# Other values for loads and engine instructions in the planner of a two-layer decoder trunk

## The chip, the cores and the metric

The kernel runs on one core of a Trainium2 chip. The metric is the device time of one execution in microseconds, the median of several runs. One further execution was recorded by the hardware profiler; all rows below come from it. PE is TensorE, DVE VectorE, ACT ScalarE, POOL GpSimd, SP SyncE; PEld is PE's loading of weights.

## What is computed

Two layers over x (1024 tokens of 1024 channels, f32), each with a mixing part and an MLP, both normalised and modulated by six vectors (shift, scale, gate, twice) that come from a conditioning vector c. The last line of the function is a final norm.

```python
for l in range(DEPTH):                                   # DEPTH = 2
    mod = (silu(c) @ w_ada[l] + b_ada[l])                # 6 x 1024
    shift1, scale1, gate1, shift2, scale2, gate2 = split(mod)
    h = rms_norm(x, g_mix_norm[l]) * (1.0 + scale1) + shift1
    p = h @ w_in[l]          # q_sb, k_sb, v_sb, q_lat, kv_lat, k_rope, gate_sb, gate_mla
    o_sb  = stick_breaking_attention(q_sb, k_sb, v_sb) @ w_sb_out[l]     # 8 heads of 64
    o_mla = softmax_attention(latent q, k, v with rope) @ w_mla_out[l]   # 8 heads
    merged = sigmoid(gate_sb) * o_sb + sigmoid(gate_mla) * o_mla
    x = x + gate1 * (merged @ w_mix_out[l])
    h = rms_norm(x, g_mlp_norm[l]) * (1.0 + scale2) + shift2
    x = x + gate2 * (square(relu(h @ w_up[l])) @ w_down[l])
```

## The kernel before

Products are made in a 32-bit float type with reduced mantissa. Each f32 operand is split into a high and a low part: ACT casts the high part, POOL or DVE subtracts it from the source for the low one, and PE sums three products (high by high, high by low, low by high). x and all hidden values lie with channels on the 128 partitions and tokens along the free dimension, in halves of 512; a product is 128 channels by 512 tokens. The MLP uses a seven-product scheme for 2 x 2 blocks in place of eight, with additions of blocks on DVE.

The stages of a layer are: modulation vectors (`mac` on DVE multiplies blocks `AD` of `w_ada` by c and adds them up in `A`; PE sums `A` over partitions), the input projection (`parts` are its split weights, `H` the split input, `lt`, `lh`, `ll` the latent vectors), attention (`sq` and `mq` are queries and keys, `sc` the scores, `W` and `F` the weights, which PE transposes into `wth` and `wtl`, `V` the values), merge and output projection, MLP up (`pr` loaded weights, `T` sums of their blocks made by `pair_weights`, `pw` their split parts, `u` and `hid` the hidden values, combined on DVE by `combine`, line 1525), and MLP down (`down`, line 1582). The values of the attention go to HBM as rows `T`, come back as `vT` by one load of 512 KB, and are transposed on PE (`make_v`, line 975).

In `down`, `operand` loads the weights `wr` (512 KB each) and eight hidden blocks `T` (256 KB each, in six buffers shared with other uses); ACT casts each `T` into `bo`, DVE subtracts for its low half and so frees the `T`. For each step and each p, DVE adds or subtracts `wr` blocks where the step needs it, ACT casts `wr` into the high `ws`, POOL subtracts for the low `ws`, and PE runs 24 products on the pair. DVE adds the result into `x`. There are 14 steps of 4 pairs in each layer, 112 pairs in all.

What sets the order: nothing is issued as it is written. `Plan.record` (line 193) notes each operation with its reads, writes, tiles and duration (`cost`, line 442). `deadlines` (line 264) lays PE's operations end to end in the order of the code and counts back from them: an operation is due when its earliest user is due, less its own duration, a latency between the engines and a margin; later tiles that will take a tile's buffer count as users too. `schedule` (line 299) then plays the program with these durations, in time: whenever an engine is free it starts, of the operations that are ready and have their buffers, the one that is due first. `emit` (line 423) issues all operations in order of their planned start. On the chip each engine runs its instructions in that order and waits on semaphores, so a planned duration never sets a time on the chip, only an order. All loads and stores go through SP's one queue, in order. All instructions carry line 218, the inner function of `record`.

Of the kernel before, what the change touches and what calls it, by code (L numbers as in the profile page):

```python
# [176 lines left out]
class Plan:  # L177
# [15 lines left out]
    def record(self, engine, method, a, k):  # L193
# [14 lines left out]
        op.early = self.early  # L208
        op.func = str(k.get("func", "")).split(".")[-1]
        op.dur = cost(op.eng, method, a, k, outs, ins)  # L210
        op.succs, op.news, op.tiles = [], [], []
        if op.eng == "PE":
# [51 lines left out]
    def deadlines(self):  # L264
        ops = self.ops
        t = 0.0
        back = []
        for op in ops:
            back.append(t)
            if op.eng == "PE":  # L270
                op.dl = t
                t += op.dur
            else:
                op.dl = None
        soft = {}
        for t_ in self.tiles:
            c = t_.cls
            if not c.slots:
                continue
        for c in {id(t_.cls): t_.cls for t_ in self.tiles if t_.cls.slots}.values():  # L280
            q = len(c.slots)
            for i in range(len(c.tiles) - q):
                nxt = c.tiles[i + q].ops[0]
                for o in c.tiles[i].ops:
                    if o < nxt:
                        soft.setdefault(o, []).append(nxt)
        for op in ops:
            for p in op.preds:
                ops[p].succs.append(op.i)
        for op in reversed(ops):  # L290
            d = back[op.i] + 60.0
            for s in op.succs + soft.get(op.i, []):
                s = ops[s]
                x = s.dl - op.dur - self.lat(op, s) - (1.2 if op.eng == "DMA" else 0.3)
                d = min(d, x)
            if op.eng != "PE":
                op.dl = d - op.early

    def schedule(self):
        self.deadlines()  # L300
        ops = self.ops
        n = len(ops)
# [52 lines left out]
        now = 0.0  # L355
        while done < n:
# [7 lines left out]
            now = heapq.heappop(events)  # L364
            while events and events[0] <= now + 1e-6:
                heapq.heappop(events)
            for e in engines:
                while free[e] <= now + 1e-6:
# [5 lines left out]
                    while av and len(skipped) < 60:  # L374
                        d, i = heapq.heappop(av)
                        op = ops[i]
# [10 lines left out]
                    op = pick  # L387
# [4 lines left out]
                    dur = op.dur  # L392
# [6 lines left out]
                    end = now + dur  # L399
                    if e == "DMA":  # L400
                        busy = max(0.46, dur)
                        end = now + 1.2 + dur
                    op.end = end
                    free[e] = now + busy
                    heapq.heappush(events, free[e])
# [8 lines left out]
                    for s in op.succs:  # L414
                        s = ops[s]
# [15 lines left out]
def width(v):  # L431
    n = 1
    if v.dims is not None:
        for a, b in [(x, y) for _, x, y in v.dims[1:]]:
            n *= b - a
        return n
    for a, b in v.box[1:]:
        n *= b - a
    return n


def cost(eng, method, a, k, outs, ins):

    if eng == "DMA":
        v = (outs + ins)[0]
        n = 1
        for x, y in v.box:
            n *= y - x
        return n * 4 / 360e3
    n = width(outs[0])  # L450
    if eng == "PE":
        dt = str(ins[0].tile.dtype)
        if "32r" in dt:
            return 0.107 if n < 16 else (n if n >= 256 else 4 * n) / 2400.0 + 0.003
        if "bfloat" in dt:
            return n / 2400.0 + 0.003
        return 0.109 if method == "transpose" else 0.13
    psum = any(getattr(v.tile.cls, "psum", False) for v in ins)
    if eng == "ACT":
        x = 0.052 if psum else 0.093  # L460
        if isinstance(k.get("bias"), View):
            x += 0.093
        if k.get("accum_out") is not None:
            x += 0.093
        return x + n / 1200.0
    if eng == "DVE":
        if method == "reduce_max":
            n = width(ins[0])
        x = 0.069 + n / 960.0
        if method == "tensor_tensor_scan":  # L470
            x += n / 960.0
        if method == "scalar_tensor_tensor" and len(ins) > 2:
            x += 0.06
        if method in ("tensor_scalar", "tensor_copy") and not psum:
            x = 0.069 + n / 1920.0 + (0.06 if len(ins) > 1 else 0)
        return x
    if method == "memset":
        return 0.036 + n / 1200.0
    if method == "tensor_scalar":
        return 0.26 + n * 3.33e-3  # L480
    return 0.15 + n * 2.1e-3


class Part:
# [1289 lines left out]
```

## Time and profile before

| | us |
|---|---|
| three runs | 3214.45, 3218.63, 3219.18 |
| median | 3218.63 |
| the profiled execution | 3226.48 |
| its span, first to last instruction | 3224.7 |
| PE busy | 3079.3 (95%) |
| DVE busy | 2242.2 (70%) |
| ACT busy | 1542.2 (48%) |
| POOL busy | 1184.0 (37%) |
| mean granted TensorE clock | 0.986 |

Busy time of an engine is time in which it has an instruction in work. A row that gives a wait counts idle time of an engine in front of an instruction, with the operation that ended last before it. The share of PE says how little of the span is not products; the rows below say where that little lies.

### The profile page before, as it was taken

Reading aid. Unit: us, or ns where it says so; the run is one execution under the profiler, and the core shown is the slowest. Engines: PE = TensorE matmul, PEld = TensorE weight load, DVE = VectorE, ACT = ScalarE, POOL = GpSimd, SP = SyncE. Lnnn points to the kernel's source line nnn. Section 1 sums busy time; section 2 is a strip of 40 time slices with the busy share of each in tenths; the row PEclk is TensorE's granted clock in tenths of the full one; section 3 lists DMA queues with packets and bytes.
Section 4 is the critical chain, followed back from the end, with each engine's and each line's share of the span. In section 5 each row is a group of like instructions: output and inputs, shape, how many; then the busy total and the mean of one; then the engine's idle time right before and its main releaser. Section 6 shows DMA issues by size and latency. Waiting matters only on the chain.

```text
span 3224.7 us, 42818 instructions
## 1 busy us (share of the span) xinstructions
PE 3079.3 (95%) x14791; PEld 2497.0 (77%) x14791; DVE 2242.2 (70%) x3246; ACT 1542.2 (48%) x2647; POOL 1184.0 (37%) x942
## 2 busy tenths in 40 slices
PE   5999999999999899999999999999999999999998
PEld 4877777888777778877777777778877777887786
DVE  7585556667667966698878636556756677559886
ACT  4443556667344444433443336556744444444343
POOL 3322444211233655344432324441113355434442
PEclk9999999999999999999999999999999999999999
DMA  6559445445843644845144764454466445476622
GB/s 220 176 184 280 142 117 138 111 106 169 273 136 111 221 164 163 280 153 184 66 140 133 246 207 131 113 143 115 121 201 195 134 141 183 150 225 212 183 85 86
DMA packets 439869, 527.20 MB, mean 163 GB/s; under 512 B 32339, under 2 KB 310501, under 8 KB 439653
## 3 DMA queue, kind: packets, MB, share of 16 engines
q1 hardware_dynamic: 439652, 524.48, 53.0%
q8 instruction: 117, 1.92, 0.2%
q14 instruction: 100, 0.81, 0.1%
HBM read 362.36 MB, written 162.00 MB: 163 GB/s over the span
## 4 chain that ended last, share of the span: by engine, by line
PE 60%; DVE 16%; DMA 12%; issue 5%; ACT 5%; POOL 1%; SPq 1%; DVEq 0%; ACTq 0%; POOLq 0%
PE pp L218 47%; PE tp L218 8%; PE sc L218 4%; DVE A L218 3%; DMA T<-dram 3%; DVE bo L218 2%; DMA dram<-T 2%; DVE T L218 2%; DMA AD<-in_w_ada 2%; DVE x L218 1%; DVE wr L218 1%; DMA dram<-lt 1%; ACT F L218 1%; ACT W L218 1%; DVE F L218 1%
## 5 line engine op out<-in xcount | busy, mean ns | idle before, releaser
L218 PE MATMUL pp<-H,parts 128*128 128x512 f32 x4000 | 1052.9, 406 | 13.6 <-DVE T L218 5.9
L218 PEld LDWEIGHTS pp<-H,parts 128*128 128x128 f32 x4000 | 733.0, 190 | 165.0 <-DVE T L218 6.8
L218 PE MATMUL pp<-bo,ws 128*128 128x512 f32 x2688 | 635.3, 397 | 19.0 <-POOL ws L218 12.6
L218 PEld LDWEIGHTS pp<-bo,ws 128*128 128x128 f32 x2688 | 506.5, 189 | 145.5 <-POOL ws L218 17.0
L218 POOL TENSOR_TENSOR parts<-raw,parts 128x1024 fp32r<-128x1024 f32 (+2 forms) x158 | 320.4, 2029 | 686.6 <-ACT parts L218 609.8
L218 POOL TENSOR_TENSOR ws<-wr,ws 128x1024 fp32r<-128x1024 f32 x112 | 298.3, 2672 | 370.2 <-ACT ws L218 352.1
L218 PE MATMUL pp<-t,pw 128*128 128x512 f32 x1344 | 322.9, 399 | 18.3 <-ACT u L218 11.2
L218 PEld LDWEIGHTS pp<-t,pw 128*128 128x128 f32 x1344 | 255.3, 191 | 80.6 <-ACT u L218 12.2
L218 DVE TENSOR_TENSOR wtl<-tp,wth 128x512 fp32r<-128x512 f32 (+3 forms) x384 | 207.3, 550 | 68.0 <-ACT wth L218 65.8
L218 DVE TENSOR_TENSOR_SCAN F<-F,sc 128x128 f32<-128x128 f32 (+7 forms) x128 | 171.2, 1347 | 109.3 <-ACT F L218 77.9
L218 ACT CAST parts<-raw 128x1024 fp32r<-128x1024 f32 (+2 forms) x158 | 140.6, 891 | 211.4 <-PE pp L218 174.6
L218 PE MATMUL pp<-b,pw 128*128 128x512 f32 x1008 | 239.7, 395 | 0.0
L218 DVE SCALAR_TENSOR_TENSOR x<-pp,const,x 128x512 f32<-128x512 f32 x256 | 180.5, 741 | 81.1 <-PE pp L218 81.1
L218 ACT CAST bo<-T 128x512 fp32r<-128x512 f32 x224 | 134.6, 619 | 206.5 <-DMA T<-dram 149.5
L218 DVE TENSOR_TENSOR bo<-T,bo 128x512 fp32r<-128x512 f32 x224 | 218.5, 1022 | 17.1 <-ACT bo L218 16.6
L218 ACT CAST wth<-tp 128x512 fp32r<-128x512 f32 (+3 forms) x384 | 181.1, 481 | 100.6 <-PE tp L218 94.4
L218 DVE SCALAR_TENSOR_TENSOR A<-AD,const,A 128x256 f32<-128x256 f32 x280 | 196.6, 702 | 45.6 <-DMA AD<-in_w_ada 40.4
L218 POOL TENSOR_TENSOR W<-W,F 128x127 f32<-128x127 f32 (+7 forms) x128 | 153.1, 1203 | 198.8 <-ACT W L218 102.3
L218 PEld LDWEIGHTS pp<-b,pw 128*128 128x128 f32 x1008 | 189.0, 188 | 45.2 <-DVE u L218 0.4
L218 POOL TENSOR_TENSOR pw<-T,pw 128x512 fp32r<-128x512 f32 x112 | 163.4, 1477 | 164.7 <-ACT pw L218 164.7
L218 PE MATMUL tp<-const,W 128*128 128x128 f32 x1152 | 183.5, 273 | 4.2 <-DVE wtl L218 4.2
L218 PE MATMUL pp<-merged,parts 128*128 128x512 f32 x768 | 182.0, 398 | 5.8 <-POOL parts L218 2.9
(155 smaller groups left out, 4534.4 us busy)
## 6 DMA issues: line engine op xcount, KB each, us to landing
T<-dram SPq DMA_DIRECT2D x352, 256.0 KB
dram<-T SPq DMA_DIRECT2D x208, 256.0 KB
dram<-u SPq DMA_DIRECT2D x92, 512.0 KB
AD<-in_w_ada SPq DMA_DIRECT2D x160, 256.0 KB
raw<-in_w_in SPq DMA_DIRECT2D x68, 512.0 KB
wr<-in_w_down SPq DMA_DIRECT2D x64, 512.0 KB
pr<-in_w_up SPq DMA_DIRECT2D x56, 512.0 KB
sq<-dram SPq DMA_DIRECT2D x96, 256.0 KB
```

Source lines behind the costliest of these rows:

```text
L218: getattr(getattr(nc, engine), method)(*[r(x) for x in a], **{n: r(x) for n, x in k.items()})
```

## The change

Eight numbers of the planner take other values: the fixed part of a transfer in `deadlines` and `schedule` (1.2 to 2.2 us), the rate of a transfer in `cost` (360 to 280 GB/s), and the fixed parts of ACT, DVE and POOL instructions. The duration of PE's operations and the latencies between engines stay.

```diff
@@ deadlines, line 294
-                x = s.dl - op.dur - self.lat(op, s) - (1.2 if op.eng == "DMA" else 0.3)
+                x = s.dl - op.dur - self.lat(op, s) - (2.2 if op.eng == "DMA" else 0.3)
@@ schedule, line 402
-                        end = now + 1.2 + dur
+                        end = now + 2.2 + dur
@@ cost, DMA, line 449
-        return n * 4 / 360e3
+        return n * 4 / 280e3
@@ cost, ACT, line 460
-        x = 0.052 if psum else 0.093
+        x = 0.13 if psum else 0.17
@@ cost, DVE, lines 469 and 475
-        x = 0.069 + n / 960.0
+        x = 0.13 + n / 960.0
...
-            x = 0.069 + n / 1920.0 + (0.06 if len(ins) > 1 else 0)
+            x = 0.13 + n / 1920.0 + (0.06 if len(ins) > 1 else 0)
@@ cost, POOL, line 481
-    return 0.15 + n * 2.1e-3
+    return 0.25 + n * 2.1e-3
```

The program has the same instructions as before but for the merging of some neighbours. Of the planner's 14775 operations on PE 6546 stand at another place in its order, on ACT 1339 of 2486, on DVE 2020 of 3246, on POOL 330 of 938, of 1763 transfers 1128. The three places below are those that the prediction speaks of. A row is one instruction: operation, output, inputs, elements, and "x2" for several alike in a row. In a name such as `ws_5414_27068` the first number is the planner's tile and is the same in both programs; the second numbers the creation and is not.

**Layer 1, down projection, ACT**, before:

```order
L218 CAST ws_5405_26932<-wr_5357_26663 128x1024
L218 CAST ws_5408_26969<-wr_5358_26711 128x1024
L218 CAST bo_5390_26978<-T_5389_26857 128x512
L218 CAST bo_5392_26985<-T_5391_26867 128x512
L218 CAST bo_5394_26991<-T_5393_26875 128x512
L218 CAST bo_5396_26997<-T_5395_26881 128x512
L218 CAST bo_5398_27003<-T_5397_26887 128x512
L218 CAST bo_5400_27009<-T_5399_26893 128x512
L218 CAST ws_5411_27021<-wr_5359_26769 128x1024
L218 CAST bo_5402_27039<-T_5401_27012 128x512
L218 CAST bo_5404_27046<-T_5403_27018 128x512
L218 CAST ws_5414_27068<-wr_5360_26809 128x1024
```

and now:

```order
L218 CAST ws_5408_26948<-wr_5358_26778 128x1024
L218 CAST ws_5411_26992<-wr_5359_26896 128x1024
L218 CAST bo_5390_27012<-T_5389_26973 128x512
L218 CAST bo_5392_27022<-T_5391_26981 128x512
L218 CAST bo_5394_27031<-T_5393_26988 128x512
L218 CAST bo_5396_27039<-T_5395_26999 128x512
L218 CAST ws_5414_27046<-wr_5360_26930 128x1024
L218 CAST bo_5398_27058<-T_5397_27008 128x512
L218 CAST bo_5400_27065<-T_5399_27017 128x512
L218 CAST bo_5402_27083<-T_5401_27044 128x512
L218 CAST bo_5404_27094<-T_5403_27055 128x512
L218 CAST ws_5433_27100<-wr_5357_26730 128x1024
```

The cast of `ws_5414` moved ahead of four casts `bo`, that of `ws_5411` ahead of all six.

**The same place, DVE**, before:

```order
L218 TENSOR_TENSOR bo_5404_27046<-T_5403_27018,bo_5404_27046 128x512
L218 TENSOR_TENSOR wr_5359_26769<-wr_5295_26359,wr_5359_26769 128x1024
L218 TENSOR_TENSOR wr_5360_26809<-wr_5296_26447,wr_5360_26809 128x1024
L218 TENSOR_TENSOR wr_5326_26521<-wr_5326_26521,wr_5358_26711 128x1024
L218 SCALAR_TENSOR_TENSOR x_5268_26532<-pp_5410_27070,const_2132_10135,x_5268_26532 128x512 x2
L218 TENSOR_TENSOR wr_5327_26558<-wr_5327_26558,wr_5359_26769 128x1024
L218 TENSOR_TENSOR wr_5328_26586<-wr_5328_26586,wr_5360_26809 128x1024
L218 TENSOR_TENSOR wr_5273_26235<-wr_5273_26235,wr_5357_26663 128x1024
L218 SCALAR_TENSOR_TENSOR x_5270_26572<-pp_5413_27116,const_2132_10135,x_5270_26572 128x512 x2
L218 TENSOR_TENSOR bo_5418_27161<-T_5417_27057,bo_5418_27161 128x512
L218 TENSOR_TENSOR bo_5420_27168<-T_5419_27063,bo_5420_27168 128x512
```

and now:

```order
L218 TENSOR_TENSOR bo_5404_27094<-T_5403_27055,bo_5404_27094 128x512
L218 SCALAR_TENSOR_TENSOR x_5268_26574<-pp_5410_27048,const_2132_10155,x_5268_26574 128x512 x2
L218 TENSOR_TENSOR wr_5359_26896<-wr_5295_26422,wr_5359_26896 128x1024
L218 TENSOR_TENSOR wr_5360_26930<-wr_5296_26487,wr_5360_26930 128x1024
L218 SCALAR_TENSOR_TENSOR x_5270_26693<-pp_5413_27096,const_2132_10155,x_5270_26693 128x512 x2
L218 TENSOR_TENSOR wr_5325_26520<-wr_5325_26520,wr_5357_26730 128x1024
L218 TENSOR_TENSOR bo_5418_27152<-T_5417_27091,bo_5418_27152 128x512
L218 TENSOR_TENSOR bo_5420_27160<-T_5419_27104,bo_5420_27160 128x512
L218 TENSOR_TENSOR wr_5326_26563<-wr_5326_26563,wr_5358_26778 128x1024
L218 SCALAR_TENSOR_TENSOR x_5272_26743<-pp_5416_27143,const_2132_10155,x_5272_26743 128x512 x2
L218 TENSOR_TENSOR bo_5422_27168<-T_5421_27111,bo_5422_27168 128x512
```

`wr_5326` moved from ahead of `bo_5418` to behind it, as did `wr_5327`, `wr_5328` and `wr_5273`, which come after these rows; `wr_5325` moved from some 25 places earlier to just ahead of it. On SP's queue the load of `wr_5505` moved from ahead of the load of `T_5429`, the source of the cast `bo_5430`, to eight places further on.

**Layer 0, attention, PE**, where the product `pp_1051` is made whose result goes to HBM and returns as `vT_1060`, before:

```order
L218 MATMUL pp_1051_4835<-H_18_658,parts_1036_4467 128x512
L218 MATMUL tp_1049_4901<-wth_1041_4747,V_914_4345 128x256 x4
L218 MATMUL tp_1049_4901<-wtl_1040_4846,V_912_4337 128x256 x4
L218 MATMUL tp_1049_4901<-wtl_1042_4776,V_914_4345 128x256 x4
L218 MATMUL pp_1051_4835<-H_19_671,parts_1035_4451 128x512 x2
L218 MATMUL pp_1051_4835<-H_19_671,parts_1036_4467 128x512
L218 MATMUL pp_1051_4835<-H_20_680,parts_1035_4451 128x512 x2
L218 MATMUL pp_1051_4835<-H_20_680,parts_1036_4467 128x512
L218 MATMUL pp_1051_4835<-H_21_703,parts_1035_4451 128x512 x2
L218 MATMUL pp_1051_4835<-H_21_703,parts_1036_4467 128x512
L218 MATMUL pp_1051_4835<-H_22_717,parts_1035_4451 128x512 x2
L218 MATMUL pp_1051_4835<-H_22_717,parts_1036_4467 128x512
```

and now, from the last product of `pp_1051`:

```order
L218 MATMUL pp_1051_4819<-H_22_713,parts_1036_4386 128x512
L218 MATMUL sc_1057_4916<-sq_1055_4728,sq_1054_4464 128x256
L218 MATMUL sc_1057_4916<-sq_1056_4751,sq_1054_4464 128x256
L218 LDWEIGHTS const_2_82
L218 MATMUL sc_1057_4916<-const_4_80,const_2_82 128x128
L218 MATMUL sc_1065_4920<-sq_1055_4728,sq_1054_4464 128x256
L218 MATMUL tp_1048_4925<-const_1_65,W_1031_4809 128x128 x4
L218 MATMUL sc_1065_4920<-sq_1056_4751,sq_1054_4464 128x256
L218 LDWEIGHTS const_2_82
L218 MATMUL sc_1065_4920<-const_4_80,const_2_82 128x128
L218 MATMUL pp_1081_4935<-H_7_298,parts_1079_4675 128x512 x2
L218 MATMUL tp_1049_4941<-wth_1039_4870,V_912_4332 128x256 x4
```

The transposes `tp_1048` and the sixteen products `tp_1049` moved from ahead of the end of `pp_1051` to behind it. The transposes of `vT_1060` follow 44 rows behind the end of `pp_1051` before, 47 now; they stand three products earlier than before.

**Layer 0, MLP up, DVE**, where the hidden blocks `u_2157`, `u_2158`, `u_2172` and `u_2173` are combined and the sums `T_2205` to `T_2208` of loaded weights `pr` are made, before:

```order
L218 TENSOR_TENSOR T_2205_10480<-pr_2203_10379,pr_2204_10450 128x512
L218 TENSOR_TENSOR T_2206_10487<-T_2205_10480,pr_2203_10379 128x512
L218 TENSOR_TENSOR T_2207_10494<-pr_2203_10379 128x512
L218 TENSOR_TENSOR u_2158_10360<-u_2158_10360,u_2157_10314 128x512
L218 TENSOR_TENSOR T_2208_10509<-pr_2204_10450,T_2206_10487 128x512
L218 TENSOR_TENSOR u_2157_10314<-u_2157_10314 128x512
L218 TENSOR_TENSOR u_2173_10474<-u_2173_10474,u_2172_10434 128x512
L218 TENSOR_TENSOR u_2157_10314<-u_2158_10360,u_2157_10314 128x512
L218 TENSOR_TENSOR u_2172_10434<-u_2172_10434 128x512
L218 TENSOR_TENSOR u_2158_10360<-u_2158_10360,u_2157_10314 128x512
L218 TENSOR_TENSOR u_2172_10434<-u_2173_10474,u_2172_10434 128x512
L218 TENSOR_TENSOR u_2173_10474<-u_2173_10474,u_2172_10434 128x512
```

and now:

```order
L218 TENSOR_TENSOR u_2158_10363<-u_2158_10363,u_2157_10313 128x512
L218 TENSOR_TENSOR u_2157_10313<-u_2157_10313 128x512
L218 TENSOR_TENSOR u_2173_10466<-u_2173_10466,u_2172_10420 128x512
L218 TENSOR_TENSOR u_2172_10420<-u_2172_10420 128x512
L218 TENSOR_TENSOR u_2157_10313<-u_2158_10363,u_2157_10313 128x512
L218 TENSOR_TENSOR u_2172_10420<-u_2173_10466,u_2172_10420 128x512
L218 TENSOR_TENSOR u_2158_10363<-u_2158_10363,u_2157_10313 128x512
L218 TENSOR_TENSOR T_2205_10545<-pr_2203_10433,pr_2204_10499 128x512
L218 TENSOR_TENSOR u_2173_10466<-u_2173_10466,u_2172_10420 128x512
L218 TENSOR_TENSOR T_2206_10552<-T_2205_10545,pr_2203_10433 128x512
L218 TENSOR_TENSOR T_2207_10554<-pr_2203_10433 128x512
L218 TENSOR_TENSOR T_2208_10558<-pr_2204_10499,T_2206_10552 128x512
```

The four steps on `T` moved behind seven of the eight steps of the combine.

**The same place, SP**, before:

```order
L218 DMA pr_2204_10450<-in_w_up 128x4x256
L218 DMA dram_2070_10462<-u_2158_10360 128x1024
L218 DMA u_2173_10474<-dram_2067_9881 128x1024
L218 DMA AD_2313_10489<-in_w_ada 128x2x256
L218 DMA dram_2070_10462<-u_2157_10314 128x512
L218 DMA pr_2230_10506<-in_w_up 128x4x256
```

and now:

```order
L218 DMA dram_2070_10450<-u_2158_10363 128x1024
L218 DMA u_2173_10466<-dram_2067_9888 128x1024
L218 DMA u_2172_10420<-dram_2067_9888 128x512
L218 DMA dram_2070_10450<-u_2157_10313 128x512
L218 DMA pr_2204_10499<-in_w_up 128x4x256
L218 DMA dram_2070_10450<-u_2157_10313 128x1024
```

The load of `pr_2204` moved from ahead of two writes of `u` and two other transfers to behind the first write of `u_2157`.

## Rows read from the trace of the kernel before

**Rows 1.** The page, busy us (share of the span) and instructions of each engine.

```profile
PE 3079.3 (95%) x14791; PEld 2497.0 (77%) x14791; DVE 2242.2 (70%) x3246; ACT 1542.2 (48%) x2647; POOL 1184.0 (37%) x942
```

**Rows 2.** Table by stretch: start:end us, length, busy us and instructions, PEclk, DMA share, GB/s.

```profile
240.00:320.00 80.00, 73.95 (x325) 59.68 (x325) 50.13 (x91) 25.52 (x49) 23.25 (x27) 0.98 0.90 277
...
2700.00:2780.00 80.00, 80.00 (x346) 64.72 (x346) 51.64 (x65) 34.75 (x49) 42.65 (x30) 1.00 0.49 167
...
2960.00:3040.00 80.00, 74.72 (x312) 59.18 (x311) 75.52 (x79) 30.06 (x40) 42.04 (x14) 0.98 0.67 201
```

**Rows 3.** Waits of PE: engine, line, waited for, us in total, times, longest us.

```profile
PE pp L218 <- POOL ws L218: 12.6, 10, 2.4
PE pp L218 <- ACT u L218: 11.2, 3, 9.2
...
PE tp L218 <- DMA vT<-dram: 10.1, 7, 2.2
PE tp L218 <- ACT A L218: 8.2, 7, 2.1
PE pp L218 <- ACT pw L218: 7.0, 2, 3.9
...
PE sc L218 <- ACT W L218: 4.9, 12, 0.6
```

**Rows 4.** Chain of waits around 530 us: start us, us, what.

```profile
520.33 1.88 PE tp L218 x16
...
530.33 6.36 DMA dram<-T
...
536.70 3.98 DMA vT<-dram
```

**Rows 5.** The tile `bo`: instructions, duration ns min/median/max, first and last start us.

```profile
L218 ACT CAST bo<-T x224: 600/621/627, 1306.7 to 3171.9; 128x512 fp32r<-128x512 f32 x112
L218 DVE TENSOR_TENSOR bo<-T,bo x224: 672/680/2926, 1307.4 to 3173.8; 128x512 fp32r<-128x512 f32 x112
```

**Rows 6.** Timeline of ACT, layer 1 down: start us, us, instruction [idle before <-releaser].

```profile
2962.70 1.32 ACT L218 CAST bo<-T 128x512 fp32r<-128x512 f32 x2 [10.84 <-DMA T<-dram]
...
2975.77 1.05 ACT L218 CAST ws<-wr 128x1024 fp32r<-128x1024 f32 x1
...
2989.83 1.37 ACT L218 CAST bo<-T 128x512 fp32r<-128x512 f32 x2 [13.01 <-DMA T<-dram]
```

**Rows 7.** Chain of waits at the same place, GpSimd's subtraction.

```profile
2992.22 3.05 POOL ws L218
```

**Rows 8.** Timeline of PE at the same place.

```profile
2968.99 3.27 PE L218 MATMUL pp<-bo,ws 128*128 128x512 f32 x13 [1.46 <-POOL ws L218]
...
2992.20 0.73 PE L218 MATMUL pp<-bo,ws 128*128 128x512 f32 x2 [1.12 <-ACT ws L218]
2995.32 2.97 PE L218 MATMUL pp<-bo,ws 128*128 128x512 f32 x7 [2.39 <-POOL ws L218]
```

**Rows 9.** Timeline of DVE at the same place.

```profile
2979.17 4.40 DVE L218 TENSOR_TENSOR wr<-wr,wr 128x1024 f32<-128x1024 f32 x3
```

**Rows 10.** Timeline of PE in attention, the transposes of `vT`.

```profile
540.73 1.09 PE L218 MATMUL tp<-const,vT 128*128 128x128 f32 x8 [1.60 <-DMA vT<-dram]
```

**Rows 11.** Timeline of PE in MLP up, layer 0.

```profile
1091.37 2.92 PE L218 MATMUL pp<-t,pw 128*128 128x512 f32 x6 [9.16 <-ACT u L218]
```

**Rows 12.** Timeline of DVE at the same place.

```profile
1078.00 0.69 DVE L218 TENSOR_TENSOR T<-pr,pr 128x512 f32<-128x512 f32 x1 [2.08 <-DMA pr<-in_w_up]
1078.72 0.69 DVE L218 TENSOR_TENSOR T<-T,pr 128x512 f32<-128x512 f32 x1
```

**Rows 13.** Timeline of SP at the same place.

```profile
1078.13 0.32 SPq L218 DMA_DIRECT2D dram<-u  x1
```

**Rows 14.** Chain of waits at the same place, the second load `pr`.

```profile
1072.19 5.79 DMA pr<-in_w_up
```

**Rows 15.** Timeline of PE at the start.

```profile
20.77 0.35 PE L218 MATMUL mods<-const,T 69*128 69x69 f32 x1 [5.34 <-DMA T<-in_g_mlp_norm]
27.66 6.71 PE L218 MATMUL pp<-const,xs 128*128 128x128 f32 x32 [6.54 <-DVE xs L218]
```

**Rows 16.** The tile `wr`, as in rows 5.

```profile
L218 DVE TENSOR_TENSOR wr<-wr,wr x64: 1207/1216/3447, 1357.5 to 3147.1; 128x1024 f32<-128x1024 f32 x64
```

## The prediction

> **What bounds the kernel now.** I read the busy times first: PE works 3079.3 us of a 3224.7 us span, DVE 70%, ScalarE 48%, GpSimd 37% [rows 1]. So TensorE sets the time, and only its idle time can be won: 3224.7 − 3079.3 = 145.4 us. The table of stretches says where that lies [rows 2]: the stretch at 2700, in the MLP, is full (346 matmuls, PE busy 80.00), that at 240, in the first projections, has 325 at a DMA share of 0.90, and that at 2960, in the second down projection, 312 with DVE busy for 75.52. Then the waits of PE, grouped by what ended them [rows 3], tell which chains are late: the split weights `ws` of the down projection (12.6 us, 10 times), the hidden `u` (11.2, one of 9.2), `vT` (10.1, 7 times), the modulation sums `A` (8.2, 7 times), the split `pw` (7.0), attention's `W` (4.9, 12 times). These six hold 54.0 us. In each case an instruction stands in its engine's queue at a place that the old durations made look safe, so the change can win by moving it, and by nothing else: it adds and removes no instruction and no byte.
>
> **How wrong the old numbers were.** A 512 KB load took 3.98 us [rows 4]; the old rule gives 1.2 + 524288/360e3 = 2.66 us, the new one 2.2 + 524288/280e3 = 4.07 us. A 128x512 cast on ScalarE took 621 ns at the median [rows 5], old 0.093 + 512/1200 = 0.520 us, new 0.597 us. The subtraction `bo<-T` of that size on DVE took 680 ns at the median [rows 5], old 0.602 us, new 0.663 us. So the planner now wants such a load 1.4 us earlier before its user and allows each ScalarE or DVE step 60 to 80 ns more. PE's own durations are unchanged.
>
> **Down projection, `ws`.** The ScalarE timeline of layer 1 [rows 6] shows how the stall arises. ScalarE idles 10.84 us in front of two `bo<-T` casts whose loads are late, and the `ws` casts stand behind these in the same queue; the same again at 2989.83 after 13.01 us of idling. GpSimd's subtraction, 3.05 us [rows 7], follows the cast, and PE stands still for 1.46 us at 2968.99, 1.12 at 2992.20 and 2.39 at 2995.32 [rows 8]. The order rows show two cures. For the first, the cast `ws_5414` moves from behind the six casts `bo_5394` to `bo_5404` to a place ahead of the four last of them, so that the late loads no longer hold it: 1.46 us go. For the second, ScalarE keeps its order (`bo_5430` before `ws_5442`), and what counts is why the load of `bo_5430` was late. Its buffer is one of six `T`, free only when DVE has done the subtraction `bo_5418`, and that stood behind three `wr` operations that took 4.40 us [rows 9]. In the new order `wr_5326`, `wr_5327`, `wr_5328` and `wr_5273` go behind `bo_5418`, `wr_5325` comes ahead of it, and on SP's queue the `wr` load ahead of it goes behind eight `T` loads. DVE reaches `bo_5418` by 4.40 us earlier (the one that enters weighs about what the fourth that leaves weighs), the load follows, then cast, split and product; PE waited 1.12 + 2.39 = 3.51 us there, so it goes. The same pair of patterns stands in layer 0 around 1400 and 1430. Of the 12.6 us and the shorter waits directly for the `ws` cast I count 11 gone; ends: 15, with those shorter waits, and 4, if only the first cure works.
>
> **Attention, `vT`.** V goes to HBM and back: 6.36 us for the write, 3.98 us for the load, then PE transposes it [rows 4], all seven waits (longest 2.2) end on that load [rows 3]. In the place shown PE waited 1.60 us [rows 10]. The new order puts the 16 products `tp_1049` and four transposes `tp_1048` behind the last `pp_1051` product instead of before it, so `pp_1051` ends 20 short matmuls earlier, at 0.12 us each (16 in 1.88 us [rows 4]) 2.4 us; the `vT` transposes move up by three products of 0.23 us (80.00/346). The lead grows by 1.7 us against a wait of 1.60 us. Over the seven places I take 8 of 10.1 us; ends 10 and 3, as the write could be slower when more transfers crowd.
>
> **MLP up, `u` and `pw`.** PE stood 9.16 us at 1091.37 [rows 11], released by ScalarE's copy into `u`, and that by DVE, which had waited 2.08 us for a load `pr` and run the four pair operations `T<-pr` among the first steps of the combine [rows 12]. In the new order seven of the eight combine steps come ahead of the four `T`. That takes the 2.08 us and four steps of 0.69 [rows 12] or more, 4.8 us, from in front of the combine's end. But on ScalarE the copy into `u` (`u_2187`) now stands behind a cast of `T_2207`, which needs the second `pr` load, and SP issues that load behind the write of `u_2157` (1078.13 [rows 13]) instead of at 1072.19. It took 5.79 us [rows 14]; from 1078.5 it lands at 1084.3, three `T` steps of 0.7 us and casts of 0.6 us make about 1087.5 to 1088.5 in place of 1091.4: 3 us. The earlier `T_2176` to `T_2179` move back behind `A` steps, and the other `pw` waits (7.0) may grow. I take −3; ends −9 (the whole wait) and +6 (`pw` waits nearly doubled).
>
> **Modulation in layer 0, `A`.** The stretch at 240 is bound by transfers (0.90) [rows 2]; earlier loads cannot help there, and `AD` loads move back by 3 to 7 rows while the `T` and `lt2` steps come earlier. I take −3 of the 8.2; ends −8 and +4 (half as much again). **`W`**: half of these twelve waits of up to 0.6 us get a longer lead; −2, ends −4 and 0.
>
> **Start.** The multiply-adds of the first chunk now run before the row statistics `ST`, where DVE waited for ScalarE, but the copy `const<-mods` stands ahead of the first `xs`, and it cannot run before PE's product at 20.77; then come `A` steps and the `rsqrt` chain, so that PE, which began on `xs` at 27.66 [rows 15], may begin up to 3 us later, while the first scale vectors are ready earlier. Of the multiply-adds that stood ahead of a wait of PE near 79, fewer stand there now. I take −2; ends −6 and +5.
>
> **Elsewhere.** Nearly half of PE's instructions change place, and places that do not wait today may. The trace cannot show these; the nearest rows are the waits that exist, 1.1 to 2.4 us each [rows 8]. Three new ones of 2 us are +6, as I take; ends 0 and +14. **Sum**: −11 − 8 − 3 − 3 − 2 − 2 + 6 = −23 us against the profiled execution of 3226.5 us (the span and 1.8 us around it, which stay), so 3203.5. That execution lies 7.9 us above the median of 3218.6, and the forecast goes from the median: 3195.6, rounded to **3196**.
>
> **Where a rule of the notes speaks against it.** The trace first: one and the same DVE operation with two SBUF inputs takes very different times, `bo<-T` 672 to 2926 ns and `wr` 1207 to 3447 ns [rows 5, 16], where the new rule always counts 0.663 and 1.197 us. *The Trainium skill, page "SBUF — State Buffer", section "Who interferes with whom", says why: VectorE and GpSimd share a port pair under an exclusive lock, and a VectorE instruction with two SBUF inputs and a GpSimd instruction that reads SBUF block one another for their whole length. By that rule the time depends on which GpSimd instruction runs beside, and no constant in the planner's table can hold it.* What it would do here is the third rival below.
>
> **Rivals.** *Nothing to measure*: the stalls shift by less than their size, or the next one in the queue takes their time; the sum keeps half of `ws` and loses the rest, 3218.6 − 5 = about 3214. For it: PE is 95% busy, and stretch 240 is bound by DMA. Against: the `ws` and `vT` leads grow by about as much as the waits. *Slower by the late `wr`*: the additions and subtractions on `wr`, moved back by 6 to 25 rows on DVE, come late for the `ws` casts that read them; then ScalarE, GpSimd and PE wait in turn. There are 112 `ws` pairs of 24 products; PE needs a new one each 24 × 0.23 = 5.5 us. Between the tightest subtraction (`wr_5359`) and its first product the program placed 38 us of PE's products before and places 16 now. Subtraction, cast and split take up to 3.45 + 1.05 + 3.05 = 7.6 us [rows 6, 7, 16], so it decides when DVE, at 75.52 of 80 us in the stretch at 2960 [rows 2], runs more than 8 us behind. If a quarter of the pairs then waited 2.39 us [rows 8], that is 28 × 2.39 = 67 us, less 12.6 of before and 20 of the other terms: +34, 3253. Against it: most of the moved operations keep 20 us and more. *The lock keeps the DVE-bound places as they are*: in the MLP and in half the `ws` places DVE's steps are of this kind, and the new table still counts the short time for them; the `u`/`pw` term falls to 0, `ws` to −5, and new waits of that kind stay at +6: 3218.6 − 5 − 8 − 3 − 2 − 2 + 6 = 3204.6. *No effect on the order*: excluded by the order rows.
>
> **Chances.** Forecast 0.52 (3180 to 3208), the lock 0.18 (3200 to 3212), nothing to measure 0.16, slower by `wr` 0.14. A measurement of this kernel can tell about 0.2%, so "same" is 3212.2 to 3225.1. Faster: 0.52 + 0.17 = 0.69; same 0.16; slower 0.15 (0.14, and a little of the start's bad end). The range 3178 to 3228 holds all but the far end of the slow rival and a sum with every term at its good end.
>
> **What would show it.** PE's waits for `ws` fall from 12.6 to under 3 and those for `vT` from 10.1 to about 2; ScalarE no longer idles over 10 us in front of a `bo` cast that has a due `ws` cast behind it; no 9 us wait at `u`; PE's idle time is about 122 us. I am wrong if PE's waits for `ws`, `wr` or `pp<-DVE` in the down stages grow (second rival), if PE starts on `xs` after 30 us, or if new waits of over 3 us stand in the modulation and merge stages.

## The result

| | before | after |
|---|---|---|
| median of six runs, us | 3214.96 | 3192.61 |
| lowest to highest | 3212.38 to 3219.18 | 3188.72 to 3194.50 |
| profiled execution | 3226.48 | 3194.19 |
| PE idle in its span | 145.4 | 120.0 |

The ratio is 0.9924, 95% interval 0.9914 to 0.9935: 22 us faster by the medians, where 23 were forecast, and the forecast of 3196 us lies 3 us off. The profiled execution of before lies 11.5 us above the median of its kernel, that of after 1.6, so differences between the two traces add up to 32 us, ten more than the change is worth. Only the size of single terms suffers from that.

The page of after, busy times:

```profile
PE 3072.4 (96%) x14791; PEld 2501.4 (78%) x14791; DVE 2237.7 (70%) x3246; ACT 1537.7 (48%) x2649; POOL 1197.5 (38%) x942
```

Waits of PE after (what is waited for, us, times, longest), to be read against [rows 3]:

```profile
PE pp L218 <- DVE lt L218: 12.4, 7, 3.0
...
PE pp L218 <- ACT u L218: 8.0, 3, 3.3
PE pp L218 <- ACT pw L218: 4.8, 2, 2.8
...
PE pp L218 <- POOL pw L218: 4.1, 2, 2.1
...
PE pp L218 <- POOL ws L218: 3.4, 2, 1.8
...
PE tp L218 <- ACT A L218: 2.5, 3, 1.1
...
PE sc L218 <- ACT W L218: 1.9, 7, 0.3
```

`ws` fell from 12.6 to 3.4 us, `A` from 8.2 to 2.5, `W` from 4.9 to 1.9, and there is no row for `vT` any more (10.1). `u` and `pw` together hardly fell (18.2 before, 16.9 now with the waits on GpSimd's half of `pw`), and waits for `lt` have grown to 12.4 us. Before, they were:

```profile
PE pp L218 <- DVE lt L218: 5.6, 3, 2.7
```

Where the time went, by stages: PE's instructions of a trace, each weighted with its dense duration (the time it takes where PE does not wait), are added up in the order in which they were issued, and the times are compared at which the same amount of work was done. The columns named e are experiments of the next section.

| until (us of before) | after | e5 | e6 | e9 | e10 |
|---|---|---|---|---|---|
| 325 start, layer 0 projections | +3.1 | +0.4 | +2.0 | −0.4 | −2.5 |
| 560 attention with `vT` | −15.7 | −5.0 | −14.6 | −15.3 | −10.5 |
| 977 rest of it, merge, output | −4.4 | −3.7 | −3.6 | −0.8 | −7.4 |
| 1319 MLP up | −3.9 | +1.3 | −1.6 | −0.1 | −6.6 |
| 1600 MLP down | −11.5 | −13.9 | −3.7 | −13.9 | −9.6 |
| 1960 layer 1 projections | +3.5 | +4.4 | +3.1 | +6.0 | −12.0 |
| 2140 attention with `vT` | −6.1 | −0.4 | −3.1 | −2.3 | −6.8 |
| 2525 rest, merge, output | +1.7 | −2.9 | −4.0 | −3.1 | −6.8 |
| 2883 MLP up | +6.8 | +0.5 | +1.4 | −1.3 | +4.8 |
| end | −5.8 | −3.4 | +0.5 | −7.8 | −4.1 |

Up to 1296 us every engine of e5 runs, by the names in the two traces, the instructions of before in their order, and yet e5 is 8.3 us less up to 977: this is what the one execution of before has too much. A single row of up to 5 us can be of this kind.

### The profile page after: what moved, and what is told of

Read it like the earlier page. It is cut to its first block, busy times and chain, and to the rows that moved or that the text cites. A ratio compares the mean times of both kernels' runs of the same rounds, so it can differ in the third digit from the quotient of the medians.

```text
span 3192.4 us, 42754 instructions
## 1 busy us (share of the span) xinstructions
PE 3072.4 (96%) x14791; PEld 2501.4 (78%) x14791; DVE 2237.7 (70%) x3246; ACT 1537.7 (48%) x2649; POOL 1197.5 (38%) x942
## 5 line engine op out<-in xcount | busy, mean ns | idle before, releaser
L218 PE MATMUL pp<-H,parts 128*128 128x512 f32 x4000 | 1043.5, 405 | 14.5 <-DVE T L218 4.7
L218 PEld LDWEIGHTS pp<-H,parts 128*128 128x128 f32 x4000 | 730.9, 190 | 165.1 <-ACT H L218 6.5
L218 PE MATMUL pp<-bo,ws 128*128 128x512 f32 x2688 | 631.2, 396 | 7.9 <-POOL ws L218 3.4
L218 PEld LDWEIGHTS pp<-bo,ws 128*128 128x128 f32 x2688 | 506.2, 189 | 130.4 <-POOL ws L218 5.3
L218 POOL TENSOR_TENSOR parts<-raw,parts 128x1024 fp32r<-128x1024 f32 (+2 forms) x158 | 322.7, 2044 | 666.6 <-ACT parts L218 626.3
L218 POOL TENSOR_TENSOR ws<-wr,ws 128x1024 fp32r<-128x1024 f32 x112 | 307.4, 2751 | 356.7 <-ACT ws L218 304.4
L218 PE MATMUL pp<-t,pw 128*128 128x512 f32 x1344 | 327.1, 402 | 16.9 <-ACT u L218 8.0
L218 PEld LDWEIGHTS pp<-t,pw 128*128 128x128 f32 x1344 | 257.6, 192 | 81.1 <-ACT u L218 9.0
L218 DVE TENSOR_TENSOR wtl<-tp,wth 128x512 fp32r<-128x512 f32 (+3 forms) x384 | 205.0, 550 | 75.8 <-ACT wth L218 72.3
L218 ACT CAST parts<-raw 128x1024 fp32r<-128x1024 f32 (+2 forms) x158 | 140.9, 893 | 235.9 <-PE pp L218 193.6
L218 DVE SCALAR_TENSOR_TENSOR x<-pp,const,x 128x512 f32<-128x512 f32 x256 | 181.0, 741 | 90.3 <-PE pp L218 89.0
L218 PE MATMUL pp<-b,pw 128*128 128x512 f32 x1008 | 238.6, 394 | 0.1
L218 DVE TENSOR_TENSOR_SCAN F<-F,sc 128x128 f32<-128x128 f32 (+7 forms) x128 | 171.9, 1348 | 82.9 <-ACT F L218 46.4
L218 POOL TENSOR_TENSOR W<-W,F 128x127 f32<-128x127 f32 (+7 forms) x128 | 153.7, 1205 | 191.9 <-ACT W L218 148.3
L218 PEld LDWEIGHTS pp<-b,pw 128*128 128x128 f32 x1008 | 189.1, 188 | 44.7 <-DVE u L218 0.5
L218 ACT CAST wth<-tp 128x512 fp32r<-128x512 f32 (+3 forms) x384 | 177.2, 483 | 93.8 <-PE tp L218 88.9
L218 DVE SCALAR_TENSOR_TENSOR A<-AD,const,A 128x256 f32<-128x256 f32 x280 | 201.8, 721 | 29.0 <-DMA AD<-in_w_ada 23.0
L218 ACT CAST ws<-wr 128x1024 fp32r<-128x1024 f32 x112 | 116.6, 1049 | 203.9 <-PE pp L218 159.8
L218 DVE TENSOR_TENSOR bo<-T,bo 128x512 fp32r<-128x512 f32 x224 | 202.5, 950 | 9.6 <-ACT bo L218 9.4
L218 POOL TENSOR_TENSOR pw<-T,pw 128x512 fp32r<-128x512 f32 x112 | 159.4, 1438 | 131.0 <-ACT pw L218 121.4
L218 DVE TENSOR_TENSOR u<-pp,u 128x512 f32<-128x512 f32 x168 | 113.1, 687 | 128.6 <-PE pp L218 126.0
L218 ACT ACTIVATE u<-u 128x1024 f32<-128x1024 f32 x112 | 118.7, 1060 | 153.3 <-DVE u L218 148.7
```

Source lines behind the costliest of these rows:

```text
L218: getattr(getattr(nc, engine), method)(*[r(x) for x in a], **{n: r(x) for n, x in k.items()})
```

## The experiments

Each was compared with the kernel before on the same chip; the median of before there lay between 3214.5 and 3215.3 us. My theory (A): the gain is a sum of places, `ws` and `vT` above all, and comes from the transfer numbers. The rivals: it comes from the engines' numbers (B); or it is the luck of one joint order, and has no parts (C).

**Which of the eight numbers.** Four kernels with a part of the diff each.

```diff
e1_transfers: lines 294, 402 (1.2 -> 2.2) and 449 (360e3 -> 280e3)
e2_engines:   lines 460, 469, 475, 481
e3_fixed:     lines 294, 402
e4_rate:      line 449
```

> Only the transfer numbers are new (fixed part 2.2 us, 280 GB/s); ACT, DVE and POOL keep the old ones. Theory A, the transfer numbers carry the gain, since the ws, vT and A chains all begin with a load: about 3196 us, PE's waits for ws near 4 us and for vT near 0, as in the changed kernel. Theory B, the engines' fixed parts carry it: about 3213 us. Theory C, no number has a share of its own and the sum is order luck: anything between 3190 and 3220, and the parts do not add up to the whole. In the planned order this kernel has the cast ws_5414 ahead of the late bo casts and the wr load behind the T loads, both as in the changed kernel.

> Only the fixed parts of ACT, DVE and POOL are new; transfers keep 1.2 us and 360 GB/s. Theory A: near 3212 us, vT still waited for by about 8 us, ws by about 9 (its order keeps ws_5414 behind the late bo casts, but has the wr load behind the T loads: the second cure without the first). Theory B: about 3195 us. Theory C: anything between 3190 and 3220.

> Only the fixed part of a transfer is new (1.2 to 2.2 us, in the due times and in the played schedule). The order in the down projection stays as in the kernel before at the place looked at, so ws should stay at 10 to 13 us; the vT transposes stand 48 rows behind the end of their product, 44 before, so vT falls to 2 us or less. If the fixed part carries the gain (theory A, first half): 3198 us. If only vT and A depend on it: 3204 us.

> Only the rate of a transfer is new (360 to 280 GB/s). The order in the down projection has both cures, so ws falls to about 4 us; the vT transposes stand 48 rows behind their product, 44 before, and since a 512 KB load is planned 0.4 us longer only, part of the vT wait, about 3 us, remains. If the rate carries the gain: 3198 us; if the two transfer numbers share it by places: 3203 us.

| | median us | ratio to before | 95% interval |
|---|---|---|---|
| e1_transfers | 3187.03 | 0.9913 | 0.9898 to 0.9928 |
| e2_engines | 3209.24 | 0.9976 | 0.9962 to 0.9990 |
| e3_fixed | 3186.84 | 0.9914 | 0.9900 to 0.9929 |
| e4_rate | 3182.49 | 0.9894 | 0.9879 to 0.9908 |

Theory A holds as to which numbers: the transfers alone give all of it, with `ws` at 3.9 us and no row for `vT` as expected, and the engines about 5 us. But the two transfer numbers do not share the gain. Each alone gives 28 or 32 us, both together 27, all eight 22. That part of theory C is true: the parts do not add. I had also expected `ws` at 10 to 13 us with the fixed part alone and at 4 with the rate alone. The waits of PE for the two, e3 first, say otherwise:

```profile
PE pp L218 <- ACT u L218: 14.5, 2, 7.5
...
PE pp L218 <- POOL ws L218: 6.9, 4, 2.7
```

```profile
PE pp L218 <- POOL ws L218: 9.0, 4, 3.0
...
PE pp L218 <- ACT u L218: 2.0, 2, 1.4
```

6.9 and 9.0: the order at one place in layer 1 doesn't tell the sum over 112 pairs. And `u` took 14.5 us in one and 2.0 in the other, with no number of the MLP's engines changed. `vT` is gone from the lists of e1, e3 and e4. But in e2, where I had expected 8 us for it and 9 for `ws`, both fell further, without any new transfer number, and a wait of 12.3 us stands there that before does not have:

```profile
PE tp L218 <- DVE const L218: 12.3, 1, 12.3
...
PE pp L218 <- POOL ws L218: 6.4, 5, 1.8
...
PE tp L218 <- DMA vT<-dram: 3.6, 4, 2.0
```

So the engines' numbers move these two places too; in time they gave little.

**One place at a time.** The kernel before, with the two new transfer numbers for some transfers only (an attribute of each operation in place of the constant):

```diff
+        new = op.eng == "DMA" and (self.new or <output is vT> and self.new_vT)
+        op.fix = 2.2 if new else 1.2
+        if new:
+            op.dur *= 360 / 280
...
e5_down_only: self.new is set while down() records
e6_vt_only:   self.new_vT, and self.new for the writes of V's rows
e9_down_vt:   both
```

> The kernel before with the new transfer numbers (2.2 us, 280 GB/s) for the transfers of the down projection alone; every other operation keeps its old numbers, and the order outside that stage stays. If the ws term is a term of its own: ws waits fall from 12.6 to 4 us or less, vT, u and A stay as before (10, 11 and 8 us), and the time falls by 9 to 12 us, to about 3204. If the gain of the whole change is a matter of the joint order: no change of more than 5 us.

> The kernel before with the new transfer numbers for the round trip of V alone (the writes of the first attention's V rows and the loads of vT). If the vT term is a term of its own: vT waits fall from 10.1 us to under 2, ws stays at about 12.6, and the time falls by 7 to 10 us, to about 3206. If PE finds no other work for the freed places, the waits come back as waits for W, sc or wth in the attention and the time falls by less than 4 us.

> The new transfer numbers for the transfers of the down projection and for the round trip of V together, everything else as before: the two local experiments in one kernel. They gave 12.5 and 16.1 us apart. If the two are terms of their own at places far apart, they add: 28 us less, about 3186, so that these two places give more than the whole change (22.4), and the rest of the change costs some 6 us. If the places share a resource or a wait: 3192 to 3200.

| | median us | ratio to before | 95% interval |
|---|---|---|---|
| e5_down_only | 3202.06 | 0.9965 | 0.9952 to 0.9979 |
| e6_vt_only | 3198.45 | 0.9955 | 0.9938 to 0.9973 |
| e9_down_vt | 3185.69 | 0.9904 | 0.9883 to 0.9925 |

Waits of PE with the down projection alone (L225 is the record helper, L218 in the other kernels):

```profile
PE tp L225 <- DMA vT<-dram: 12.4, 8, 3.5
PE pp L225 <- ACT u L225: 11.4, 3, 9.3
...
PE pp L225 <- POOL ws L225: 4.9, 4, 1.9
```

and with the round trip of V alone, and one row of its PE timeline in the down projection:

```profile
PE pp L225 <- POOL ws L225: 12.0, 9, 2.4
...
PE pp L225 <- ACT u L225: 10.1, 3, 7.8
...
PE sc L225 <- ACT W L225: 0.9, 2, 0.4
```

```profile
2969.82 5.37 PE L225 MATMUL pp<-bo,ws 128*128 128x512 f32 x22 [2.39 <-POOL ws L225]
```

The edits are local: in the trace of e5 158 of PE's 14791 places hold another instruction than before, all around 1930 us, and in that of e6 1778, all in or next to the two attentions. e6 takes all of its own wait away and e5 most of it, and each leaves the other's and `u` about where they were; in e6 the wait of 2.39 us of [rows 8] stands at the same product, in e5 that for `vT` has 12.4 us. e6 gave 16.1 us where I had expected 7 to 10, e5 12.5 where I had expected 9 to 12. Both together give 29.6 us of the medians, and e9's waits have 2.5 us for `ws` and none for `vT`:

```profile
PE pp L225 <- ACT u L225: 10.6, 2, 9.2
...
PE pp L225 <- POOL ws L225: 2.5, 2, 1.6
```

As far as the intervals tell, they add. So these two places are terms of their own, and they carry the gain. By the medians they give more than the whole change, and the other operations that it reorders cost some 7 us on balance; but the intervals, 24 to 38 us for e9 and 21 to 28 for the change, overlap, so this cost is likely and not shown.

**Truer numbers elsewhere.** If the gain came from numbers nearer to the trace, more of them should give more. e8 is the rate alone with PE's products at 0.232 us; e11 is the changed kernel with times near the traced means for DVE instructions whose two inputs both lie in SBUF and not in PSUM, where the products `pp` of PE lie.

```diff
e8_rate_pe:
-            return 0.107 if n < 16 else (n if n >= 256 else 4 * n) / 2400.0 + 0.003
+            return 0.107 if n < 16 else (n if n >= 256 else 4 * n) / 2240.0 + 0.003
e11_two_inputs:
+        if method in ("tensor_add", "tensor_sub", "tensor_mul") and not psum:
+            x = 0.13 + n / 600.0
+        if method == "scalar_tensor_tensor" and not psum:
+            x = 0.13 + n / 450.0
```

> The rate of a transfer at 280 GB/s and PE's products of 512 columns at 0.232 us, which the trace shows, in place of 0.216. If a planner with a truer clock plans better: 3172 to 3182 us. If a longer PE time makes every load look safe again (PE time between two operations is planned longer, so loads and casts start later against products): ws and vT return in part, 3190 to 3205 us; its order has ws_5414 behind the late bo casts again, which speaks for this one.

> The changed kernel with longer planned times for DVE instructions with two SBUF inputs, near the means of its trace (bo 0.95, u 1.2, wr 1.7 us: 0.13 + n/600 in place of 0.13 + n/960; A 0.70 in place of 0.46). If the third rival's mechanism (the planner counts 0.66 us where the trace has 1.0 to 1.7) limits the gain: the waits for u, pw and ws fall and the time is 3180 to 3186. If a constant cannot hold it, or the old one does no harm: 3190 to 3200, no better than the changed kernel.

e8: 3230.76 us, ratio 1.0057 (1.0039 to 1.0075), 48 us more than the rate alone. e11: 3237.31 us, 1.0063 (1.0043 to 1.0083), 45 us more than the changed kernel. Of both expectations only the direction of the second half held, and the losses are larger; in e8 `ws` and `vT` did not return (7.3 us, 9.0 with the rate alone, and no row). PE's waits in e8:

```profile
PE pp L218 <- POOL parts L218: 19.6, 6, 8.1
...
PE sc L218 <- ACT W L218: 9.3, 21, 1.2
PE sc L218 <- DVE F L218: 9.3, 19, 0.7
```

PE's waits in e11, and two stretches of its table (columns as in [rows 2]):

```profile
PE pp L218 <- DVE lt L218: 31.8, 8, 6.9
PE pp L218 <- ACT u L218: 21.4, 4, 6.2
```

```profile
1280.00:1440.00 160.00, 160.00 (x691) 129.53 (x690) 121.35 (x131) 67.10 (x92) 71.31 (x31) 1.00 0.66 216
1440.00:1600.00 160.00, 160.00 (x692) 129.72 (x691) 150.77 (x150) 65.77 (x92) 76.08 (x29) 1.00 0.42 135
...
160.00:320.00 160.00, 140.71 (x586) 112.65 (x584) 106.21 (x185) 63.60 (x111) 39.47 (x37) 0.90 0.61 197
```

In e8 the waits are spread over several chains (`parts` 19.6 us, `W` 9.3, `F` 9.3), as if every product came a little early. In e11 the down projection of layer 0 is full, 160.00 of 160 us twice. That this is the doing of the longer times is not shown: by the measure of the stage table the row of layer 0's MLP down has −18.0 us in e11, and −17.7 in e12 below, which does not have these times. PE waits 31.8 us for `lt` and 21.4 for `u`, and in the first projections it is idle for 19 of 160 us. Why the longer times do that no run here settles.

**A small step and the best of the parts.** e7 is the rate alone at 250 GB/s, e12 the changed kernel at 284 in place of 280, e10 the rate of 280 for all transfers with the fixed part of 2.2 us only in the down projection and for V.

```diff
e7_rate250:     -        return n * 4 / 360e3
                +        return n * 4 / 250e3
e12_rate284:    -        return n * 4 / 280e3
                +        return n * 4 / 284e3
e10_rate_local: e9_down_vt, and op.dur *= 360 / 280 for every transfer
```

> Only the rate of a transfer is new, at 250 GB/s in place of the 280 of the rate experiment (3182.5 us). If what counts is that loads are planned longer: equal to the rate at 280 or a little better, 3178 to 3186 us. If a good part of that result is order luck: 3188 to 3205 us.

> The changed kernel with 284 GB/s in place of 280: a change of 1.4% in one number, which makes no place safer or less safe by more than 0.03 us a load. If the time follows from what the numbers mean: 3190 to 3195, as the changed kernel's 3192.6. If a good part of a few us is order luck: off by 4 us or more to either side.

> 280 GB/s for all transfers, the fixed part of 2.2 us only in the down projection and the round trip of V, engines as before. The rate alone gave 3182.5 with 9.0 us of waits for ws. If the local term adds to it: ws falls to 4 or 5 and the time to about 3178. If the order elsewhere is shuffled by it: 3180 to 3192.

e7: 3185.67 us, 0.9914 (0.9895 to 0.9934), an interval that overlaps with that of e4: going from 280 on to 250 gave nothing more. e12: 3189.91, 0.9916 (0.9898 to 0.9935), not to be told from the changed kernel, so a small step in a number doesn't throw the time about by tens of us; its waits for `lt` (15.7 us) are there too. e10: **3165.64**, 0.9840 (0.9819 to 0.9861), 27 us faster than the changed kernel and the fastest here. Its waits and page:

```profile
PE pp L225 <- POOL ws L225: 6.9, 5, 2.0
PE pp L225 <- ACT pw L225: 6.4, 2, 3.3
...
PE pp L225 <- ACT u L225: 2.2, 2, 1.6
...
PE 3054.7 (97%) x14791; PEld 2492.0 (79%) x14791; DVE 2232.0 (71%) x3246; ACT 1543.5 (49%) x2647; POOL 1188.6 (38%) x942
```

It is also 12 us faster than I had expected at best, and my reason for it was wrong: `ws` fell to 6.9 us from the 9.0 of the rate alone, not to 4, and the stage table has its surplus over the change in layer 1's projections (−12.0, as +3.5 for the change) and in the merge stages, where its numbers are those of the rate alone and the trace of e4 is as good (−11.3 in those projections). The 11 us between the traces of e4 and e10 are spread, at most 4 in one stage. That it is the fastest is measured; that its numbers are the right ones is not shown.

## Why the prediction was right

**Down projection (−11): right, in the main also in how.** ACT and PE at the place of [rows 6, 8], in after:

```profile
2945.85 1.05 ACT L218 CAST ws<-wr 128x1024 fp32r<-128x1024 f32 x1 [0.59 <-PE pp L218]
2953.54 1.31 ACT L218 CAST bo<-T 128x512 fp32r<-128x512 f32 x2 [6.65 <-DMA T<-dram]
2954.76 1.04 ACT L218 CAST ws<-wr 128x1024 fp32r<-128x1024 f32 x1
```

```profile
2949.80 16.41 PE L218 MATMUL pp<-bo,ws 128*128 128x512 f32 x70
```

ACT still stands before two `bo` casts, for 6.65 us in place of 13.01, the `ws` cast follows at 2954.76, and PE runs 70 products through with no wait. The other place of the pair has none either. The local experiment gives 12.5 us for the whole term (7 to 15 by its interval). Two signs did not come in full: `ws` has 3.4 us and not under 3, and ACT still idles 10.23 and 11.05 us before `bo` casts at 2979.42 and 3003.33 with `ws` casts behind them. PE does not wait there, so what went is the lateness of the `ws` casts and not ACT's idling. That late additions on `wr` would cost more than this (the second rival, whose own price of 3253 us the stated range left out) did not come about: 16 us of products between the tightest one and its user were enough.

**`vT` (−8) and `W` (−2): right, and too small.** PE and SP at the place of [rows 10], in after:

```profile
520.90 0.54 SPq L218 DMA_DIRECT2D vT<-dram  x1
```

```profile
526.96 1.03 PE L218 MATMUL tp<-const,vT 128*128 128x128 f32 x8
```

The load is issued 6.1 us before the transposes, where it was 4.0, and PE doesn't wait. All seven waits went, not four fifths of them, and with those for `W` gone in part e6 has 16.1 us. The waits themselves were 10.1 + 4.9 us. So the term was mis-sized, mostly by taking a share of it for crowding that did not show; what is left, about 1 us, lies inside e6's interval (9 to 20 us).

**MLP up (−3): the place right, the term wrong.** The wait of 9.16 us for `u` [rows 11] is gone; PE idles 1.48 us there, for DVE's step `const<-tp,const`. That is better than the 5 to 6 us that the step left of it: the second `pr` load and the combine were both done sooner than I laid them. Three steps of the combine, before and after:

```profile
1088.91 4.56 DVE L218 TENSOR_TENSOR u<-u,u 128x512 f32<-128x512 f32 x3
```

```profile
1063.35 1.89 DVE L218 TENSOR_TENSOR u<-u,u 128x512 f32<-128x512 f32 x3
```

The first three ran beside GpSimd's subtractions, the other three while GpSimd was idle. But other waits grew, in both layers (the first row is the one of 1.48 us):

```profile
1068.46 0.24 PE L218 MATMUL tp<-const,A 128*128 128x2 f32 x1 [1.48 <-DVE const L218]
...
1112.41 4.40 PE L218 MATMUL pp<-t,pw 128*128 128x512 f32 x12 [3.15 <-ACT u L218]
...
2575.00 1.91 PE L218 MATMUL pp<-t,pw 128*128 128x512 f32 x5 [2.81 <-ACT pw L218]
...
2671.35 4.61 PE L218 MATMUL pp<-t,pw 128*128 128x512 f32 x12 [3.29 <-ACT u L218]
```

At the products of 1112.41 and 2671.35 PE had waited 1.42 and 0.65 us before; at 2575.00 it had waited 3.91, and now a second wait, of 2.10 us for GpSimd's half, follows the one shown. So the waits for `u` other than the long one grew from 2.1 to 8.0 us, and those for `pw` from 7.0 to 8.9. By stages the two MLP halves come to −3.9 and +6.8. The step that failed is that I costed the one long wait and put "`pw` waits may grow" into the bound only. Ahead of the wait of 3.15 us the combine now runs beside `pw`, on DVE and on POOL:

```profile
1106.73 5.01 DVE L218 TENSOR_TENSOR u<-u,u 128x512 f32<-128x512 f32 x3
```

```profile
1106.11 3.42 POOL L218 TENSOR_TENSOR pw<-pr,pw 128x512 fp32r<-128x512 f32 x2
```

**`A` (−3): the waits moved.** `A` fell by 5.7 us, `lt` rose by 6.8. DVE and PE in the projections of layer 0, after:

```profile
237.12 5.21 DVE L218 SCALAR_TENSOR_TENSOR A<-AD,const,A 128x256 f32<-128x256 f32 x4
242.36 1.39 DVE L218 TENSOR_TENSOR lt<-pp,cs 64x512 f32<-64x512 f32 x2
```

```profile
243.81 0.50 PE L218 MATMUL pp<-lh,parts 128*128 128x512 f32 x1 [1.84 <-DVE lt L218]
...
250.58 0.79 PE L218 MATMUL pp<-lh,parts 128*128 128x512 f32 x1 [2.90 <-DVE lt L218]
```

Four multiply-adds of `A` take 5.21 us, beside GpSimd (one alone takes 0.48), ahead of the step that takes products out of `pp` into `lt`, where before one or two stood between two of these; PE gets its `A` in time and waits 1.84 and 2.90 us for `lt`. I had asked only what becomes of the wait that was there, not what the instruction that is moved ahead stands in front of. **Start (−2):** PE began on `xs` at 28.05, not up to 3 us later than 27.66, and at 108 us of before the same work was done 4.7 us sooner; e5, whose order there is that of before, has 2.1 of this too.

**Elsewhere (+6): near, but not measured by itself.** I put it down to new waits at random places; by the medians of e9 and the change, what is reordered outside the two places costs some 7 us, MLP and `lt` among it. In the terms of the sum: the two places gave 29.6 us where I had 21, and all the rest cost 7 where I had it give 2. So the sum was nearer than its terms: that the two errors cancelled is luck.

**The reason behind all of it was too simple.** "The old numbers were wrong" carried the forecast. e8 and e11 put in numbers that are nearer to the trace and lose 16 and 22 us against the kernel before. A planned time sets an order and a margin, no time. PE's products planned 7% short and loads planned longer both bring operands early, and that is what the waits were in want of; this reading fits e3, e4 and e8, does not say why more of the same (e1, e7) gains no more, and was not tested by itself.

**The third rival: wrong for `ws`, near for the MLP.** The `ws` waits went, but the `u` and `pw` term came out near the 0 that it gave. That longer constants made the time worse (e11) does not speak against it, as the prediction has it that no constant can hold such a time. The DVE rows of [rows 5, 16] vary by factors of about four and three, and a count over the whole trace of before shows what goes with it. The 142 subtractions `bo<-T,bo` that no GpSimd instruction overlaps took 0.67 to 0.69 us; the 82 that one overlaps took 0.67 to 2.93, 1.61 on average. For `wr<-wr,wr` it is 1.21 to 1.23 us (33) and 1.21 to 3.45 (31). `x<-pp,const,x`, with one input in PSUM, took 0.73 to 0.75 us in both cases (143 and 113). *The rule of the Trainium skill (page "SBUF — State Buffer", section "Who interferes with whom") on the port pair that VectorE and GpSimd share bears on those rows; the counts agree with it, but no run here took the GpSimd work away from beside them, so that this is read from traces and not from an experiment.*

## What to carry to other kernels

In a list-scheduled kernel, read the waits of the bounding engine by what ended them, and go to the order at each: a change of numbers helps where it moves an instruction from behind a late load. Give such places their numbers locally and measure each by itself; here two places carried the gain, and by the medians the global change gave part of it back. A number nearer to the trace is not for that reason better, so each is tried alone, PE's too. Where the times of one instruction spread widely, look at what runs beside the long ones: here it was GpSimd, and a longer constant for all of them (e11) made the kernel slower.

## What the runs showed of the hardware

Here waits of PE cost more than their idle time. Around the two waits for `lt`, the table of after reads:

```profile
240.00:250.00 10.00, 5.12 (x19) 3.32 (x17) 9.42 (x17) 2.17 (x7) 5.26 (x8) 0.75 0.71 225
250.00:260.00 10.00, 8.73 (x24) 6.61 (x25) 5.09 (x11) 3.38 (x8) 2.21 (x3) 0.57 0.73 242
260.00:270.00 10.00, 10.00 (x47) 8.22 (x46) 6.58 (x14) 1.52 (x4) 0.88 (x1) 1.00 0.76 247
```

The granted clock is 0.57 from 250 to 260 us. Read 2 us at a time, it is 0.50, the lower of its two levels of 1.2 and 2.4 GHz, in every stretch from 246 to 258, behind the wait of 1.84 us and through that of 2.90, and 1.00 again from 260. From 250 to 260 us 24 matmuls start with PE busy for 8.73 us, where the next 10 us hold 47. The first product after the wait lasts 0.79 us, those later in the stage 0.40. PE's busy time, for the same instructions, tends to be less where its idle time is less: 3079.3 us with 145.4 of idling before, 3054.7 with 108.7 in e10 (a span of 3163.4). The three traces with the most idle time (before, e8, e11) have 3078.7 to 3080.1 us, the other eleven 3054.7 to 3072.4; within the eleven the order does not hold throughout. How much of the 24.6 us between before and e10 is the clock (0.986 and 0.991 on average) stays open.
